# A two-level seven-product matmul on one core: the second level taken out

## The chip, the cores and the metric

One Trainium2 chip, one of its cores. The metric is device time in microseconds of one execution. The kernel before has a median of 891.07 us in 3 runs (890.15 to 894.06). One execution was also profiled; all rows below come from it.

## What is computed

One layer of a hybrid encoder block over 1024 tokens of width 1024. The part that the change touches is the input projection, a 1024 x 7200 matrix:

```
h = rmsnorm(x, norm_g)
proj = einsum('bsd,de->bse', h, w_in)
(q, k, v, z_a, lr_f, lr_b, b_gate, c_gate, h_c, z_c) = split(proj)
o   = gla_direction(q, k, v, g_f) + flipped gla_direction(... g_b)   # 4 heads, chunks of 64
y_a = rmsnorm(o) * silu(z_a)
y_c = b_gate * (conv3(c_gate * h_c) + conv_b) * silu(z_c)
out = rmsnorm(x + einsum('bse,ed->bsd', concat(y_a, y_c), w_out))
```

## The kernel before, in words

The program has four stages. First x is scaled, transposed and split into float32r high and low parts, the blocks `hb[d][s]` (d: half of the 1024 input columns, s: half of the 1024 tokens), and head 0 and 1 of v are multiplied directly. Second, `value_pair` (L468) multiplies heads 2 and 3 of v. Third, the loop at L687 to L694 multiplies everything else in 12 "quads": 8 for the convolution (c_gate and h_c, then z_c and b_gate), 4 for attention (q and k, then z). Fourth come attention and the output projection, from L698 on.

Every product of two float32 matrices is made of three float32r matmuls, high by high, high by low and low by high (`product`, L392), so a product over four blocks of 128 input columns takes 12 matmuls, each with a 128x128 weight block and 512 tokens moving (a "wide" matmul).

The input projection uses a seven-product scheme (Winograd's form of Strassen's). A pair (`pair`, L417) takes two blocks of 128 output columns, e = 0 and 1, in which `a00` and `a01` are the two halves of the input columns of block 0 (tile `raw0`) and `a10`, `a11` those of block 1 (`raw1`). Sums of these weights (`comb`, L421: `s1`, `s2` and two in `tmp` tiles) and sums of the blocks `hb` (`t1` to `t4`, made once) are multiplied. VectorE adds the products out of PSUM with `plus` (L444, at L445). ScalarE rounds each weight part to its high half (L153), GpSimd subtracts to get the low half (L154); `part` (L207) does both, into a ring of 6 tiles for each half. SyncE's queue loads the weights (L82), 4 raw tiles in all, and stores results; it takes its entries in order.

One of a pair's seven products, `a01` by `b10`, goes straight into the result `c00` = `a00` by `b00` + `a01` by `b10`. In the kernel before, this product has a second level: `quad` (L558) takes two pairs at once, whose `a01` together form a matrix of 512 input columns by 256 output columns, and `second` (L519) applies the same seven-product scheme to it, with the quarters of the block `hb[1][0]` and three quarter sums of it (`tt1`, `tt2`, `tt3`, made in `later_sums` at L668 to L675 and behind `value_pair` at L680 to L685). These seven products have 256 tokens moving (a "narrow" matmul) and 2 blocks of input columns, so 6 narrow matmuls each, 42 in a quad. Their results are the tiles `r`, which each pair adds to its first product (L458).

`second` holds four PSUM banks `bx`, `by`, `bz`, `bw` of a rotation of six (`bank6`, L401: names pa, pb, pc, two of each). `bx`, `by` and `bw` are used twice. The sixth narrow product writes `by` again, so PE must wait until VectorE has read the first result out of it at L542; the fifth must wait for ScalarE's copy at L540:

```
        product(by, first_(o1), t2, True, True)
        V.tensor_tensor(p1, by, p1, ALU.add)
        ...
        product(by, o3, t4, True, True)
        V.tensor_tensor(r[1][:, lo], by, u, ALU.add)
```

Behind each convolution quad come the gates of one head and direction (`gates`, L582): 4 wide matmuls over 64 rows (L591), then ScalarE and VectorE work on them. The scheduler of the language sets each engine's order; VectorE, ScalarE, GpSimd and the DMA queue run what stands in that order, one after the other.

Of the kernel before, what the change touches and what calls it, by code (L numbers as in the profile page):

```python
# [37 lines left out]
def tile_hybrid_gla_shortconv(ctx, tc, x, norm_g, w_in, w_gk_f, b_gk_f, w_gk_b, b_gk_b,  # L38
# [168 lines left out]
    def part(src, e_lo=G, late=False):  # L207
        pool, name, bufs = (resp, "w", 2) if late else (ws, "a", 6)
        hi, lo = (pool.tile([P, 4, P], F32R, name=f"{name}_{i}", bufs=bufs) for i in ("hi", "lo"))
        hi, lo = (a[:, 0:src.shape[1]] for a in (hi, lo))  # L210
        split(hi, lo, src, A, e_lo)
        return hi, lo
# [140 lines left out]
    def less(f, x, y, blk, behind):  # L353
        V.tensor_tensor(f, x, y, ALU.subtract)
        split_later(behind, *blk, f)


    quarters = [tuple(a[:, 2 * d:2 * d + 2, 256 * s_:256 * s_ + 256] for a in hb[1][0])
                for d in range(2) for s_ in range(2)]
    tt1 = tuple(a.rearrange("p c t -> p (c t)").rearrange("p (c t) -> p c t", c=2) for a in y_pair())  # L360
    tt2, tt3 = (tuple(tp.tile([P, 2, 256], F32R, name=f"tt{i}_{n}") for n in ("hi", "lo")) for i in (2, 3))

    beside = sums()
    with tc.manual_schedule():
        for _ in values(1, wv):
# [26 lines left out]
    def product(ps, a, b_, start, stop):  # L392
        n = a[0].shape[1]
        for k in range(n):
            for j, (x0, x1) in enumerate(((0, 0), (0, 1), (1, 0))):
                T.matmul(ps, a[x0][:, k], b_[x1][:, k], start=start and k == 0 and j == 0,  # L396
                         stop=stop and k == n - 1 and j == 2, skip_group_check=not start)
# [7 lines left out]
    def load(col):  # L405
        return weights(w_in[:, :, col:col + P])
# [7 lines left out]
            with tc.issue_after(behind.ins):  # L414
                beside.pop(0)()

    def pair(raw0, raw1, take, c2=None, mid=None, step=lambda behind: None):  # L417

        a00, a01, a10, a11 = raw0[:, 0:4], raw0[:, 4:8], raw1[:, 0:4], raw1[:, 4:8]

        def comb(f, x0, x1, op):  # L421
            V.tensor_tensor(f, x0, x1, op)  # L422
            return f

        def t4_():
            return tmp().rearrange("p (c e) -> p c e", e=P)

        o00 = part(a00)
        if c2 is None:
            o01 = part(a01)  # L430
        s1 = comb(s_tile(), a10, a11, ALU.add)
        s2 = comb(s_tile(), s1, a00, ALU.subtract)
        os2 = part(s2)
        os3 = part(comb(t4_(), a00, a10, ALU.subtract))
        os1 = part(s1)
        o11 = part(a11)
        os4 = part(comb(t4_(), a01, s2, ALU.subtract))

        def whole_product(a, b_):
            ps = bank6()  # L440
            product(ps, a, b_, True, True)
            return ps

        def plus(f, ps, x):  # L444
            step(V.tensor_tensor(f, ps, x, ALU.add))  # L445
            return f

        pa = whole_product(o00, b00)
        p1 = tmp()
        A.copy(p1, pa)  # L450
        if mid is not None:
            mid()
        if c2 is None:
            product(pa, o01, b10, False, True)
            c2 = tmp()
            A.copy(c2, pa)
        else:
            V.tensor_tensor(c2, pa, c2, ALU.add)  # L458
        take(0, 0, c2)
        plus(p1, whole_product(os2, t2), p1)  # L460
        w = plus(tmp(), whole_product(os3, t3), p1)
        p5 = whole_product(os1, t1)
        take(1, 1, plus(tmp(), p5, w))
        plus(p1, p5, p1)
        take(1, 0, plus(w, whole_product(o11, t4), w))
        take(0, 1, plus(p1, whole_product(os4, b11), p1))
# [49 lines left out]
            V.tensor_tensor(x[i], ps, x[i], ALU.add)  # L516
            out_v(h0, 1, i, x[i])

    def second(x, y, h):  # L519

        b00, t1, t2, t3, b10, b11, t4 = h
        a00, a01, a10, a11 = x[:, 0:2], x[:, 2:4], y[:, 0:2], y[:, 2:4]
        f, g = s_tile(), s_tile()
        s2, s1, s3, s4 = f[:, 0:2], f[:, 2:4], g[:, 0:2], g[:, 2:4]
        o0 = part(x)
        V.tensor_tensor(s1, a10, a11, ALU.add)
        V.tensor_tensor(s2, s1, a00, ALU.subtract)
        o1 = part(f)
        V.tensor_tensor(s3, a00, a10, ALU.subtract)
        V.tensor_tensor(s4, a01, s2, ALU.subtract)  # L530
        o2 = part(g)
        o3 = part(a11)
        first_, last_ = (lambda o: tuple(a[:, 0:2] for a in o)), (lambda o: tuple(a[:, 2:4] for a in o))
        r = [wk.tile([P, 512], F32, name="r2", bufs=2) for _ in range(2)]
        lo, hi = slice(0, 256), slice(256, 512)
        w = tmp()
        p1, u = w[:, lo], w[:, hi]
        bx, by, bz, bw = (bank6()[:, lo] for _ in range(4))
        product(bx, first_(o0), b00, True, True)
        A.copy(p1, bx)  # L540
        product(by, first_(o1), t2, True, True)
        V.tensor_tensor(p1, by, p1, ALU.add)  # L542
        product(bz, first_(o2), t3, True, True)
        V.tensor_tensor(u, bz, p1, ALU.add)
        product(bw, last_(o1), t1, True, True)
        V.tensor_tensor(r[1][:, hi], bw, u, ALU.add)
        product(bx, last_(o0), b10, False, True)
        A.copy(r[0][:, lo], bx)
        product(by, o3, t4, True, True)
        V.tensor_tensor(r[1][:, lo], by, u, ALU.add)  # L550

        def finish():
            product(bw, last_(o2), b11, False, True)
            V.tensor_tensor(r[0][:, hi], bw, p1, ALU.add)

        return *r, finish

    def quad(cols_a, take_a, cols_b, take_b):  # L558
        xa, xb = load(cols_a[0]), load(cols_b[0])
        ra, rb, finish = second(xa[:, 4:8], xb[:, 4:8], h2)  # L560
        pair(xa, load(cols_a[1]), take_a, ra, finish, step)
        pair(xb, load(cols_b[1]), take_b, rb)

    def to_dram(dsts):
        def take(e, half, ap):
# [93 lines left out]
    def later_sums():  # L659

        behind = []
        for c in range(4):
            f = joined(t2, c, tmp)
            minus(joined(hb[1][0], c, tmp), f, t4, c, f, behind)
            if c % 2 == 1:
                yield
        finish_low(behind)
        f = [tmp().rearrange("p (c t) -> p c t", c=2) for _ in range(3)]  # L668
        for f_, i in zip(f, (0, 1, 3)):
            whole(f_, quarters[i])  # L670
        less(f[0], f[1], f[0], tt1, behind)
        yield
        less(f[1], f[2], f[1], tt3, behind)
        less(f[0], f[2], f[0], tt2, behind)
        finish_low(behind)  # L675
        yield

    with tc.issue_after(last_mm[0].ins):
        value_pair(2, 3, o00, o01, os2, a00, a01, a10, a11, s2, later_sums())
    f = [wk.tile([P, 512], F32, name="r2", bufs=2).rearrange("p (c e) -> p c e", c=2) for _ in range(2)]  # L680
    whole(f[0], tt2)
    whole(f[1], quarters[2])
    V.tensor_tensor(f[0], f[1], f[0], ALU.subtract)
    split(*quarters[1], f[0])
    h2 = quarters[0], tt1, tt2, tt3, quarters[2], quarters[3], quarters[1]  # L685

    for j in range(CW // P):  # L687
        u, *first_ = conv_u(j)
        args = *first_, *conv_y(j, u)
# [378 lines left out]
```

## Time and profile before

| | |
|---|---|
| median of 3 runs | 891.07 us (890.15 to 894.06) |
| the profiled execution, its own time | 889.61 us |
| its span, first to last instruction | 887.9 us |
| TensorE (PE) matmuls busy | 860.0 us, 97% |
| VectorE (DVE) busy | 704.4 us, 79% |
| ScalarE (ACT) busy | 393.7 us, 44% |
| GpSimd (POOL) busy | 421.6 us, 47% |
| mean granted TensorE clock | 0.995 |

In the profile a matmul's bar reaches from its start to its modelled end, and a matmul starts before the one ahead of it has ended. So the time that a matmul costs in a full stream is read from the distance between two starts, not from the length of a bar; and the idle time printed behind a row, in brackets, is counted from the modelled end of the matmul ahead. PEld are the weight loads, which run beside the matmuls. A row with "<-" names what the engine waited for. Times are in us from the span's start.

### The profile page before, as it was taken

The page shows a single profiled execution, that of the slowest core. Times are in us where ns is not written, and L with a number is a line of the kernel's source. Part 1 is how long each engine was busy: PE and PEld are TensorE (multiplying, and loading weights), DVE is VectorE, ACT ScalarE, POOL GpSimd, SP SyncE. Part 2 cuts the span into 40 slices and gives each one's busy share as a digit, 9 for nine tenths or more (in the row PEclk, how much of TensorE's full clock was granted, in tenths as well). Part 3 has the DMA queues.
Part 4 walks back from the last instruction along what each step waited for, and adds up shares of the span by engine and source line. Part 5 has one row for each costly group of instructions (what it writes and reads, how often), then busy time and mean ns, then how long its engine had stood idle before and what let it go on. Part 6 is the DMA issues. An engine that isn't in the chain of part 4 may idle for free.

```text
span 887.9 us, 12975 instructions
## 1 busy us (share of the span) xinstructions
PE 860.0 (97%) x4452; PEld 722.8 (81%) x4452; DVE 704.4 (79%) x1301; ACT 393.7 (44%) x823; POOL 421.6 (47%) x374
## 2 busy tenths in 40 slices
PE   7999989999999999999999999999999999999996
PEld 6999978887787878788878888887878787888885
DVE  5889968788888798888887566667799989975754
ACT  4634323454636263444544233433455446542453
POOL 3423657586767675766766554520112222222231
PEclk9999999999999999999999999999999999999998
DMA  8511331223132322222244433469665434410122
GB/s 301 115 54 49 96 120 48 82 62 118 49 95 72 96 66 77 72 72 72 72 132 129 131 96 105 135 210 392 226 205 190 131 113 135 131 37 24 42 78 95
DMA packets 102164, 100.35 MB, mean 113 GB/s; under 512 B 10705, under 2 KB 82385, under 8 KB 101586
## 3 DMA queue, kind: packets, MB, share of 16 engines
q1 hardware_dynamic: 102098, 99.53, 35.4%
q8 instruction: 35, 0.57, 0.3%
q14 instruction: 31, 0.25, 0.1%
HBM read 71.20 MB, written 28.31 MB: 112 GB/s over the span
## 4 chain that ended last, share of the span: by engine, by line
PE 76%; DVE 17%; issue 3%; DMA 2%; ACT 1%; SPq 0%; POOLq 0%; POOL 0%; DVEq 0%; ACTq 0%
PE out L734 16%; PE pa L396 16%; PE pb L396 15%; PE pc L396 15%; PE po L891 4%; PE out L223 3%; PE pu L936 2%; DVE tmp L445 1%; DVE tmp L649 1%; DVE s L422 1%; DVE tmp L320 1%; DMA b<-b_dram 1%; PE out L291 1%; DMA xt<-in_x 1%; PE pk L928 1%
## 5 line engine op out<-in xcount | busy, mean ns | idle before, releaser
L154 POOL TENSOR_TENSOR a_lo<-s,a_hi 128x512 fp32r<-128x512 f32 x74 | 116.2, 1575 | 54.8 <-ACT a_hi L153 54.5
L154 POOL TENSOR_TENSOR a_lo<-raw,a_hi 128x512 fp32r<-128x512 f32 x84 | 111.0, 1325 | 22.1 <-ACT a_hi L153 18.4
L154 POOL TENSOR_TENSOR a_lo<-tmp,a_hi 128x512 fp32r<-128x512 f32 x48 | 70.3, 1464 | 103.9 <-ACT a_hi L153 84.6
L148 POOL TENSOR_TENSOR rs<-rs,mhalf 128x1 f32<-128x1 f32 x48 | 28.7, 598 | 143.1 <-DVE rs L147 135.7
L734 PE MATMUL out<-a_hi,y_hi 128*128 128x512 f32 x192 | 88.7, 462 | 0.5 <-ACT y_hi L153 0.5
L153 ACT CAST a_hi<-raw 128x512 fp32r<-128x512 f32 x108 | 63.8, 596 | 56.4 <-PE pc L396 15.1
L153 ACT CAST a_hi<-tmp 128x512 fp32r<-128x512 f32 x48 | 29.8, 620 | 120.2 <-DVE tmp L422 98.9
L734 PE MATMUL out<-a_hi,y_lo 128*128 128x512 f32 x192 | 77.0, 401 | 0.0
L734 PE MATMUL out<-a_lo,y_hi 128*128 128x512 f32 x192 | 76.8, 400 | 0.0
L846 POOL TENSOR_TENSOR kt<-kt,k 128x256 f32<-128x256 f32 x32 | 26.3, 822 | 95.5 <-ACT kt L843 72.2
L153 ACT CAST a_hi<-s 128x512 fp32r<-128x512 f32 x74 | 45.0, 617 | 50.7 <-PE pa L396 17.5
L396 PE MATMUL pb<-h_hi,a_hi 128*128 128x512 f32 (+1 forms) x128 | 48.3, 377 | 4.8 <-DVE tmp L542 4.2
L396 PE MATMUL pc<-h_hi,a_hi 128*128 128x512 f32 (+1 forms) x128 | 47.6, 372 | 2.9 <-DVE tmp L542 2.6
L396 PE MATMUL pa<-h_hi,a_hi 128*128 128x512 f32 (+1 forms) x128 | 47.6, 372 | 2.8 <-DVE tmp L542 2.8
L396 PE MATMUL pb<-h_lo,a_hi 128*128 128x512 f32 (+1 forms) x128 | 47.1, 368 | 0.0
L396 PE MATMUL pb<-h_hi,a_lo 128*128 128x512 f32 (+1 forms) x128 | 47.0, 367 | 0.0
L396 PE MATMUL pa<-h_lo,a_hi 128*128 128x512 f32 (+1 forms) x128 | 46.6, 364 | 0.0
L396 PE MATMUL pc<-h_lo,a_hi 128*128 128x512 f32 (+1 forms) x128 | 46.6, 364 | 0.0
L396 PE MATMUL pc<-h_hi,a_lo 128*128 128x512 f32 (+1 forms) x128 | 46.5, 363 | 0.0
L396 PE MATMUL pa<-h_hi,a_lo 128*128 128x512 f32 (+1 forms) x128 | 46.5, 363 | 0.0
L736 DVE TENSOR_TENSOR res<-out,res 128x512 f32<-128x512 f32 x48 | 32.9, 686 | 12.4 <-PE out L734 12.4
L734 PEld LDWEIGHTS out<-a_hi,y_lo 128*128 128x128 f32 x192 | 36.3, 189 | 7.8
(341 smaller groups left out, 2696.6 us busy)
## 6 DMA issues: line engine op xcount, KB each, us to landing
raw<-in_w_in SPq DMA_DIRECT2D x56, 512.0 KB, 3.9
raw<-in_w_out SPq DMA_DIRECT2D x16, 512.0 KB, 3.8
xt<-in_x SPq DMA_DIRECT2D x8, 512.0 KB, 8.2
yc_dram<-tmp SPq DMA_DIRECT2D x16, 256.0 KB, 2.0
b_dram<-u SPq DMA_DIRECT2D x8, 512.0 KB, 2.6
z_dram<-tmp SPq DMA_DIRECT2D x16, 256.0 KB, 2.6
s<-yc_dram SPq DMA_DIRECT2D x16, 256.0 KB, 3.9
raw<-in_x SPq DMA_DIRECT2D x8, 512.0 KB, 6.3
```

Of the source, the lines that this page charges most:

```text
L148: G.tensor_tensor(rs, rs, mhalf, ALU.pow)
L153: (e_hi.copy if e_hi is A else e_hi.tensor_copy)(hi, src)
L154: e_lo.tensor_tensor(lo, src, hi.bitcast(F32), ALU.subtract)
L223: last_mm[0] = T.matmul(ps, h_tile(a, c, t), wv[c // 4][w_][:, c % 4, :], start=part == 0 and c == 0, stop=part == 2 and c == ND - 1)
L291: T.matmul(lps, lrw[:, c, :], hb[c // 4][half][j][:, c % 4, :], start=c == 0 and j == 0, stop=c == ND - 1 and j == 1)
L320: V.tensor_tensor(f, blk[0].bitcast(F32)[:, c], blk[1].bitcast(F32)[:, c], ALU.add)
L396: T.matmul(ps, a[x0][:, k], b_[x1][:, k], start=start and k == 0 and j == 0, stop=stop and k == n - 1 and j == 2, skip_group_check=not start)
L734: T.matmul(ps, a[:, j, :], w, start=j == 0 and i == 0, stop=j == 3 and i == 2)
L736: V.tensor_tensor(res[t][:, cs], ps, (xr if row0 == NT else res[t])[:, cs], ALU.add)
L846: G.tensor_tensor(kk, kk, k4, ALU.mult)
L891: T.matmul(o, l, m, start=j == 0, stop=j == len(mm) - 1)
L936: T.matmul(pu[:, d], ks[:, d], r["v"][:, t], start=True, stop=True)
```

## The change

`second` goes, with the quarters, the quarter sums `tt1` to `tt3`, and the tiles `r`. Each pair makes `a01` by `b10` itself, as one product of 12 wide matmuls in a bank of its own from the rotation, and VectorE adds it to `p1`, the ScalarE copy of the first product. With it each pair splits its own `a01` (`o01`).

```
-    quarters = [tuple(a[:, 2 * d:2 * d + 2, 256 * s_:256 * s_ + 256] for a in hb[1][0])
-                for d in range(2) for s_ in range(2)]
-    tt1 = ...
-    tt2, tt3 = (tuple(tp.tile([P, 2, 256], F32R, ...
...
         o00 = part(a00)
-        if c2 is None:
-            o01 = part(a01)
+        o01 = part(a01)
...
         pa = whole_product(o00, b00)
         p1 = tmp()
         A.copy(p1, pa)
-        if mid is not None:
-            mid()
-        if c2 is None:
-            product(pa, o01, b10, False, True)
-            c2 = tmp()
-            A.copy(c2, pa)
-        else:
-            V.tensor_tensor(c2, pa, c2, ALU.add)
-        take(0, 0, c2)
+        c00 = tmp()
+        V.tensor_tensor(c00, whole_product(o01, b10), p1, ALU.add)
+        take(0, 0, c00)
...
-    def second(x, y, h):
...
     def quad(cols_a, take_a, cols_b, take_b):
         xa, xb = load(cols_a[0]), load(cols_b[0])
-        ra, rb, finish = second(xa[:, 4:8], xb[:, 4:8], h2)
-        pair(xa, load(cols_a[1]), take_a, ra, finish, step)
-        pair(xb, load(cols_b[1]), take_b, rb)
+        pair(xa, load(cols_a[1]), take_a, step)
+        pair(xb, load(cols_b[1]), take_b)
...
         finish_low(behind)
-        f = [tmp().rearrange("p (c t) -> p c t", c=2) for _ in range(3)]
-        for f_, i in zip(f, (0, 1, 3)):
-            whole(f_, quarters[i])
-        less(f[0], f[1], f[0], tt1, behind)
         yield
-        less(f[1], f[2], f[1], tt3, behind)
-        less(f[0], f[2], f[0], tt2, behind)
-        finish_low(behind)
...
-    f = [wk.tile([P, 512], F32, name="r2", bufs=2).rearrange("p (c e) -> p c e", c=2) for _ in range(2)]
-    whole(f[0], tt2)
-    whole(f[1], quarters[2])
-    V.tensor_tensor(f[0], f[1], f[0], ALU.subtract)
-    split(*quarters[1], f[0])
-    h2 = quarters[0], tt1, tt2, tt3, quarters[2], quarters[3], quarters[1]
```

The scheduler then sets the engines' orders anew. Three places show what moves. The first is VectorE at the end of the first convolution quad, where the second begins. In the kernel before (L445 adds products, L593 reads the gates out of PSUM, L648 and L649 finish the gated output, L422 are the weight sums, and L542, L544, L546 read the narrow products):

```order
L445 TENSOR_TENSOR tmp<-pc,tmp 128x512
L445 TENSOR_TENSOR tmp<-pa,tmp 128x512
L593 TENSOR_SCALAR u<-out,bgk 128x512
L648 SCALAR_TENSOR_TENSOR th<-th,tmp 128x512
L593 TENSOR_SCALAR u<-out,bgk 128x512
L649 SCALAR_TENSOR_TENSOR tmp<-th,tmp 128x512
L542 TENSOR_TENSOR tmp<-pc,tmp 128x256
L422 TENSOR_TENSOR tmp<-raw 128x512
L544 TENSOR_TENSOR tmp<-pa,tmp 128x256
L422 TENSOR_TENSOR tmp<-raw,s 128x512
L546 TENSOR_TENSOR r_1865<-pb,tmp 128x256
```

The same place in the changed kernel (its L540, L595, L596 are L593, L648, L649 of before; its L438 and L445 add products, L558 and L552 are the scan of the gates):

```order
L438 TENSOR_TENSOR tmp<-pa,tmp 128x512
L438 TENSOR_TENSOR tmp<-pb,tmp 128x512
L540 TENSOR_SCALAR u<-out,bgk 128x512
L595 SCALAR_TENSOR_TENSOR th<-th,tmp 128x512
L540 TENSOR_SCALAR u<-out,bgk 128x512
L596 SCALAR_TENSOR_TENSOR tmp<-th,tmp 128x512
L445 TENSOR_TENSOR tmp<-pa,tmp 128x512
L438 TENSOR_TENSOR tmp<-pb,tmp 128x512
L558 TENSOR_TENSOR u<-u 128x512
```

The gate and output work stands where it stood. What comes behind it is no longer the read of a bank that PE needs for its sixth narrow product, but the add of the quad's second wide product.

The second place is VectorE near the end of `value_pair`. In the kernel before (L499, L503, L506 add products of `value_pair`; L351, L354, L329, L334 make the quarter sums; L526 begins `second`):

```order
L499 TENSOR_TENSOR tmp<-pb,tmp 128x512
L354 TENSOR_TENSOR tmp<-tmp 128x512
L329 TENSOR_TENSOR y_lo<-tmp,y_hi 128x512
L503 TENSOR_TENSOR tmp<-pc,tmp 128x512
L354 TENSOR_TENSOR tmp<-tmp 128x512
L329 TENSOR_TENSOR tt_lo<-tmp,tt_hi 128x512
L503 TENSOR_TENSOR tmp<-pa,tmp 128x512
L334 TENSOR_TENSOR tt_lo<-tmp,tt_hi 128x512
L506 TENSOR_TENSOR tmp<-pb,tmp 128x512
L351 TENSOR_TENSOR r_1461<-tt_hi,tt_lo 128x512
L351 TENSOR_TENSOR r_1462<-h_hi,h_lo 128x512
L526 TENSOR_TENSOR s<-raw 128x256
```

In the changed kernel (its L486, L490, L493 are L499, L503, L506 of before, its L416 is L422):

```order
L486 TENSOR_TENSOR tmp<-pb,tmp 128x512
L334 TENSOR_TENSOR h_lo<-tmp,h_hi 128x512
L490 TENSOR_TENSOR tmp<-pc,tmp 128x512
L490 TENSOR_TENSOR tmp<-pa,tmp 128x512
L493 TENSOR_TENSOR tmp<-pb,tmp 128x512
L416 TENSOR_TENSOR s<-raw 128x512
L416 TENSOR_TENSOR s<-s,raw 128x512
L493 TENSOR_TENSOR tmp<-pc,tmp 128x512
```

The quarter sums are gone, and the first weight sums of the first quad have moved ahead, to between the adds of the fourth product of `value_pair`.

The third place is SyncE's DMA queue around the end of the first quad. In the kernel before (L654 stores the gated convolution, L613 the gates, L82 loads weights):

```order
L654 DMA yc_dram<-tmp 128x512 x2
L82 DMA raw<-in_w_in 128x8x128 x2
L613 DMA b_dram_79<-u 128x1024
L82 DMA raw<-in_w_in 128x8x128 x2
L654 DMA yc_dram<-tmp 128x512 x2
```

In the changed kernel (L601 and L560 are the two stores):

```order
L601 DMA yc_dram<-tmp 128x512
L82 DMA raw<-in_w_in 128x8x128
L601 DMA yc_dram<-tmp 128x512
L560 DMA b_dram_79<-u 128x1024
L82 DMA raw<-in_w_in 128x8x128 x3
```

One of the two loads that stood behind both stores now stands between them, the other ahead of them, and the store of the gates has three loads behind it, of which the third is for one quad later.

## Rows read from the trace of the kernel before

**Rows 1.** The page: busy time of the engines; DMA issues of weights (us to landing).
```profile
PE 860.0 (97%) x4452; PEld 722.8 (81%) x4452; DVE 704.4 (79%) x1301; ACT 393.7 (44%) x823; POOL 421.6 (47%) x374
...
raw<-in_w_in SPq DMA_DIRECT2D x56, 512.0 KB, 3.9
```

**Rows 2.** The chain in order of time: start, length, what; second convolution quad, then attention.
```profile
200.91 3.72 PE pa L396 x18
...
208.09 2.75 PE pc L396 x12
...
241.65 3.73 PE pb L396 x18
...
484.25 3.67 PE pb L396 x18
...
522.37 3.60 PE pc L396 x18
```

**Rows 3.** PE's timeline, start of the second convolution quad: start, length, what, [idle before].
```profile
194.73 0.40 PE L396 MATMUL pb<-h_hi,a_lo 128*128 128x512 f32 x1
...
196.17 0.39 PE L396 MATMUL pc<-h_hi,a_hi 128*128 128x256 f32 x1
...
196.87 0.28 PE L396 MATMUL pc<-h_hi,a_lo 128*128 128x256 f32 x1
196.99 0.28 PE L396 MATMUL pa<-tt_hi,a_hi 128*128 128x256 f32 x1
...
199.12 0.28 PE L396 MATMUL pc<-h_hi,a_hi 128*128 128x256 f32 x1
...
199.72 0.28 PE L396 MATMUL pc<-h_hi,a_lo 128*128 128x256 f32 x1
200.91 0.39 PE L396 MATMUL pa<-h_hi,a_hi 128*128 128x256 f32 x1 [0.92 <-DVE tmp L542]
201.14 0.28 PE L396 MATMUL pa<-h_lo,a_hi 128*128 128x256 f32 x1
```

**Rows 4.** DVE's timeline at the same place, and at the end of `value_pair`.
```profile
199.39 1.14 DVE L649 SCALAR_TENSOR_TENSOR tmp<-th,tmp 128x512 f32<-128x512 f32 x1
200.45 0.41 DVE L542 TENSOR_TENSOR tmp<-pa,tmp 128x256 f32<-128x256 f32 x1
...
118.43 0.41 DVE L542 TENSOR_TENSOR tmp<-pb,tmp 128x256 f32<-128x256 f32 x1
```

**Rows 5.** PE's timeline: end of `value_pair`, first quad; then the first matmul behind the last quad.
```profile
110.92 0.28 PE L479 MATMUL pc<-a_lo,h_hi 128*128 128x256 f32 x1
...
113.05 0.28 PE L396 MATMUL pb<-tt_hi,a_lo 128*128 128x256 f32 x1
114.23 0.36 PE L396 MATMUL pc<-tt_hi,a_hi 128*128 128x256 f32 x1 [0.90 <-ACT a_hi L153]
...
116.30 0.28 PE L396 MATMUL pa<-h_hi,a_lo 128*128 128x256 f32 x1
118.89 0.58 PE L396 MATMUL pb<-h_hi,a_hi 128*128 128x256 f32 x1 [2.32 <-DVE tmp L542]
...
594.76 0.39 PE L734 MATMUL out<-a_hi,y_hi 128*128 128x512 f32 x1
```

**Rows 6.** Stretches: length, busy us of PE, PEld, DVE, ACT, POOL, granted clock, DMA share, GB/s.
```profile
118.50:123.00 4.50, 4.11 (x15) 3.62 (x16) 3.14 (x6) 1.54 (x4) 4.24 (x3) 0.62 0.56 152
119.00:592.00 473.00, 464.79 (x2222) 385.44 (x2223) 366.99 (x493) 202.48 (x333) 310.40 (x232) 1.00 0.31 92
```

**Rows 7.** Groups of DVE: xcount | busy us, mean ns | idle before; the quarter sums.
```profile
L354 DVE TENSOR_TENSOR tmp<-tmp 128x512 f32<-128x512 f32 x3 | 2.5, 845 | 0.0
L351 DVE TENSOR_TENSOR tmp<-h_hi,h_lo 128x512 f32<-128x512 f32 x3 | 2.3, 809 | 0.0
```

**Rows 8.** Groups of POOL on the page: low halves of the weights.
```profile
L154 POOL TENSOR_TENSOR a_lo<-s,a_hi 128x512 fp32r<-128x512 f32 x74 | 116.2, 1575 | 54.8 <-ACT a_hi L153 54.5
```

**Rows 9.** Waits of DVE: us in total, times, longest.
```profile
DVE s L526 <- DMA raw<-in_w_in: 15.1, 10, 3.4
```

More of the change, by code (lines that the diff above doesn't have):

```diff
@@ L355, in less @@
         split_later(behind, *blk, f)
-    quarters = [tuple(a[:, 2 * d:2 * d + 2, 256 * s_:256 * s_ + 256] for a in hb[1][0])
-                for d in range(2) for s_ in range(2)]
-    tt1 = tuple(a.rearrange("p c t -> p (c t)").rearrange("p (c t) -> p c t", c=2) for a in y_pair())
-    tt2, tt3 = (tuple(tp.tile([P, 2, 256], F32R, name=f"tt{i}_{n}") for n in ("hi", "lo")) for i in (2, 3))
     beside = sums()
@@ L415, in step, with pair @@
                 beside.pop(0)()
-    def pair(raw0, raw1, take, c2=None, mid=None, step=lambda behind: None):
+    def pair(raw0, raw1, take, step=lambda behind: None):
         a00, a01, a10, a11 = raw0[:, 0:4], raw0[:, 4:8], raw1[:, 0:4], raw1[:, 4:8]
@@ L517, in value_pair @@
             out_v(h0, 1, i, x[i])
-    def second(x, y, h):
[L521 to L556, printed above, removed]
     def quad(cols_a, take_a, cols_b, take_b):
         xa, xb = load(cols_a[0]), load(cols_b[0])
-        ra, rb, finish = second(xa[:, 4:8], xb[:, 4:8], h2)
-        pair(xa, load(cols_a[1]), take_a, ra, finish, step)
-        pair(xb, load(cols_b[1]), take_b, rb)
+        pair(xa, load(cols_a[1]), take_a, step)
+        pair(xb, load(cols_b[1]), take_b)
     def to_dram(dsts):
```

## The prediction

> **What bounds the kernel now.** I read the engines' busy times first. PE's matmuls are busy for 97% of the span [rows 1], so a change is worth what it does to PE's stream: the matmuls in it and the gaps between them. But a bar is longer than the step to the next start, so 97% hides gaps. I then read the chain of waits in order of time. From the first quad to the last it consists of PE's products, 2.75 us for each one of 12 wide matmuls [rows 2], broken at each convolution quad by a piece of VectorE work. PE's timeline at such a break [rows 3] shows the price of a matmul and of the wait. Twelve wide matmuls in 2.75 us are 0.229 us each. From 196.99 to 199.12 stand 18 narrow ones, 0.118 us each: half the columns, half the time. Then PE starts nothing from 199.72 to 200.91, and what it waits for is L542 on VectorE. VectorE's timeline [rows 4] says why: L542 stands behind the gate and output work, the last of it L649 at 199.39, and comes at 200.45. The bank that it reads was full at about 197.70 (the product's first matmul at 196.99 and six steps of 0.118). So VectorE was 2.8 us behind, and `second` wants the bank back after only three other narrow products, 3 x 6 x 0.118 = 2.1 us.
>
> The first quad is worse [rows 5]: 1.18 us from 113.05 to 114.23 and 2.59 us from 116.30 to 118.89, where a step of 0.118 was due. After the second of these waits the granted clock is 0.62 in the stretch from 118.5 to 123 [rows 6], so part of it ran at 1.2 GHz instead of 2.4; the engine had stood idle just before.
>
> **The change, part by part.** *Products.* A quad loses 42 narrow matmuls, 42 x 0.118 = 4.96 us, and gains 24 wide ones, 24 x 0.229 = 5.50 us [rows 2, 3]. That is 0.54 us more in each of 12 quads, 6.5 us in all, and it lies wholly on the path, since PE is the path. A bound from below is nothing less than this: both steps are measured in this stage at the same clock.
>
> For a stream of weight loads and matmuls the Trainium skill's page "TensorE: Matmul & The Clock Gate", section "Back-to-back issue gap", gives about 81 ns for 128 columns and about 131 ns for 512. On a line between them a narrow matmul is an estimated 98 ns, and the exchange would save 1.0 us in a quad instead of costing something. The trace disagrees: 229 ns for 512 columns and 118 for 256, nearly in proportion.
>
> *Waits.* The reuse of `bx`, `by` and `bw` goes, and with it both waits, for L542 and for L540. Each product now has its own bank out of six, and a bank comes round after five other products, 5 x 2.75 = 13.75 us, where VectorE was 2.8 us behind. I put the new bank wait at nothing. Its cover is those 13.75 us; with no cover at all it would again cost about what the old one did.
>
> *Quarter sums.* Near the end of `value_pair` VectorE loses six wide sums worth 2.5 + 2.3 us [rows 7] and the splits and sums that follow them. PE waits there for VectorE (118.43 for the first L542 [rows 4]), and the order shows the weight sums of the first quad moved ahead into `value_pair`. That is more than the two waits of 1.06 and 2.47 us that PE has there, so I let them go. If this cover is too thin, the first quad keeps some 5 us, with the slow clock.
>
> *Splits and adds.* In a quad the four splits of `second` give way to two, its four weight sums and its narrow evictions go, and the two adds of its results become two adds of `p1`. VectorE is busy 367 of 473 us of this stage and GpSimd 310 [rows 6], and both get less to do, so this costs nothing; PE's 2.75 us for a product covers a split of 1.58 us [rows 8]. No gain is put down for it either.
>
> *Loads.* The queue carries the same bytes. The order of loads and stores shifts, but loads still stand about a quad ahead, near 40 us, and land in 3.9 us [rows 1]. Cost nothing; the bound is a rival below.
>
> *The sum* is made over the whole stretch, because that counts every wait once. The first product could start at 110.92 + 0.12 = 111.04, and the first matmul behind the quads starts at 594.76 [rows 5]: 483.7 us now. After: 12 quads of 14 products, 168 x 2.75 = 462.0 us. To it come eight sets of gates; from 194.73 to 196.17 such a set takes 1.44 us less the 0.23 of the matmul ahead [rows 3], so 8 x 1.21 = 9.7 us. Together 471.7 us, which is 12.0 us less. As 6.5 us of matmuls are added, the waits that go must be worth 18.5 us. A check by quads: a convolution quad takes 241.65 - 200.91 = 40.74 us and would take 14 x 2.75 + 1.21 = 39.71; an attention quad takes 522.37 - 484.25 = 38.12 us and would take 38.50 [rows 2]. So the convolution quads gain a microsecond each, the attention quads, which hardly wait, lose 0.4, and the largest single piece, near 5 us, is the first quad. The rest of the program starts earlier and is otherwise left as it is.
>
> The profiled execution took 889.61 us, so its sum is 877.6. The median of the runs lies 1.46 us above that execution, and I keep this distance: **879.1 us**.
>
> **Rivals.**
>
> *The loads come late.* VectorE already waits 15.1 us in 10 times for the weights of the next quad, at most 3.4 [rows 9], and PE doesn't notice, since parts are made ahead. With a load between two stores, and three behind the store of the gates, the wait could pass on to PE. At 1.5 us in each of eight convolution quads it takes 12 us, and the time is 891. For it speaks the moved order, against it the lead of a quad. It decides when a load is issued less than its 3.9 us and a sum and split ahead of need.
>
> *VectorE's backlog only moves.* This is the case on the slow side. If PE's waits are not the banks' but VectorE's own lateness at a quad's end, then the first product whose bank still holds an unread result waits in place of the narrow one, the 18.5 us come back, and the 6.5 us of added matmuls are all that is left: 891.1 + 6.5 = 897.6 us. The place is the third or fourth product behind the gates. It needs VectorE to be over 13.75 us late, and the rows show 2.8; for it speaks that the gates and the output work still stand ahead of the first adds in VectorE's order.
>
> *The first quad keeps its waits.* VectorE reaches the first L542 only at 118.43 [rows 4], 7 us after `value_pair`; if the weight sums still come late, 5 us stay: 884.1 us.
>
> *Wide and narrow matmuls cost the same in the new order.* If weight loads set the pace, each at 0.118 us, a quad would save 18 x 0.118 = 2.1 us on products instead of paying 0.54, and the time would be 879.1 - 32 = 847 us. The wide products of the same stage, at 0.229, speak against it. The page named above would have it partly so.
>
> That the change doesn't do what it says is excluded: the order of the changed program has the wide matmuls in the place of the narrow ones.
>
> **How the numbers follow.** The forecast gets 0.85, late loads 0.05, the moved backlog 0.04, the first quad's waits 0.05, equal cost of matmuls 0.01. The range: gates could cost as little as four plain steps, 0.92 us, which takes off 2.3 us, and the runs reach 0.9 us below their median: 875.5 at the low end. At the high end stands the first quad's rival with a little scatter: 884.5. A measurement of this kernel can tell about 0.5% from no change, 4.5 us, so faster means under 886.6. Faster: 0.85 + 0.05 + 0.01 = 0.91; no change: 0.05; slower: 0.04.
>
> **What would show it.** Right: in the profile after, PE has 216 matmuls fewer, the chain of waits runs through the quads as products of 2.75 us without VectorE pieces, conv quads are 39.7 us apart and attention quads 38.5, no wait of PE names L542 or its successor, and the granted clock no longer falls at the first quad. Wrong: a new wait of PE behind the gates, on a weight part or a bank; a product that takes longer than 2.75 us; or a last stage that is longer than before and gives the gain back.

## The result and the profile after

The changed kernel takes 879.61 us (median of 4 runs, 879.14 to 880.01). The kernel before, on the same chip, takes 892.57 us (4 runs, 890.15 to 894.13). The ratio is 0.9849, interval 0.9822 to 0.9876. Predicted were 879.1 us. The profiled execution after took 879.14 us, with a span of 877.4 us.

The page after, first the busy times (as in [rows 1]), then the share of the chain by engine:

```profile
PE 859.9 (98%) x4236; PEld 713.9 (81%) x4236; DVE 644.3 (73%) x1181; ACT 374.1 (43%) x771; POOL 396.2 (45%) x349
...
PE 90%; DVE 5%; DMA 3%; issue 1%; ACT 1%; SPq 0%; POOLq 0%; POOL 0%; DVEq 0%; ACTq 0%
```

PE has 4452 - 4236 = 216 matmuls fewer and is busy for the same 860 us, so its busy time does not show the change: bars overlap, they count none of the pauses, and before they also hold slow steps and slow first matmuls behind waits. VectorE lost 60 us of work.

The chain in order of time, the rows that answer to [rows 2] (start, length, what):

```profile
111.70 2.77 PE pa L390 x12
114.47 2.75 PE pb L390 x12
...
191.08 2.97 PE pb L390 x12
194.05 2.75 PE pc L390 x12
...
230.88 2.95 PE pa L390 x12
...
270.66 2.97 PE pc L390 x12
...
578.37 2.75 PE pb L390 x12
581.11 2.75 PE pc L390 x12
583.86 4.50 PE out L667 x20
```

No piece of VectorE stands between the quads any more. Convolution quads are 39.80 and 39.78 us apart. A product behind the gates has 2.95 to 2.97 us in the chain, which counts to the modelled end of a matmul; from its first start to that of the next product it takes 2.86 to 2.88. The other products keep 2.75.

PE's waits after, with the largest total first (us in total, times, longest). None of them is at a quad's line, L390:

```profile
PE po L824 <- DVE at L811: 3.0, 9, 0.8
PE pc L237 <- POOL mask_b L120: 2.3, 1, 2.3
PE pa L185 <- DVE xt L178: 1.4, 1, 1.4
```

Stretches of the trace after (columns as in [rows 6]): the first quad's beginning, the whole quad stage, the rest:

```profile
118.50:123.00 4.50, 4.50 (x21) 3.69 (x20) 0.95 (x2) 1.06 (x2) 1.85 (x2) 1.00 0.00 0
111.50:583.70 472.20, 472.20 (x2051) 383.60 (x2049) 324.02 (x393) 187.83 (x291) 286.81 (x210) 1.00 0.32 95
583.70:877.40 293.70, 281.72 (x1369) 229.31 (x1367) 231.83 (x659) 138.06 (x393) 63.26 (x88) 1.00 0.41 139
```

The stage from the first product to the first matmul behind the quads takes 472.2 us, in which PE is busy all the time and the granted clock is 1.00. Before it was 483.6 (from the first product at 111.19), and the clock at the first quad 0.62.

Where the 11.4 us went is read from PE's timelines, from the first product of a quad to the first product of the next. The gates lie within. All lengths are in us. The runs of the experiments stand in the same table, and its last column gives the shortest and the longest of six quads:

| kernel | median | first quad | second | third to eighth |
|---|---|---|---|---|
| before | 892.4 | 44.75 | 40.23 | 40.43 to 41.25 |
| changed | 879.61 | 39.68 | 39.79 | 39.78 to 39.80 |
| e2_no_quarter_sums | 887.22 | 39.75 | 40.19 | 40.43 to 41.04 |
| e1_own_bank | 888.42 | 42.57 | 39.24 | 40.16 to 41.52 |
| e10_bank_and_no_sums | 884.66 | 39.11 | 39.23 | 40.11 to 40.88 |
| e6_first_quad_alone | 891.12 | 39.68 | 46.44 | 39.61 to 40.80 |
| e4_quarter_sums_kept | 878.81 | 39.68 | 39.79 | 39.78 to 39.80 |
| e3_same_bank | 894.46 | 39.99 | 40.12 | 41.73 to 41.77 |
| e13_four_banks | 879.86 | 39.68 | 39.84 | 39.79 to 40.14 |
| e14_two_banks | 921.86 | 42.42 | 46.16 | 44.55 to 44.60 |

The median of before is that of 23 runs. From 44.75 to 39.68 the first quad gains 5.1 us. The next seven together gain 6.4 (284.97 before, 278.53 after), and the four attention quads together lose 0.1 (153.85 and 153.95).

### The profile page after: what moved, and what is told of

Same layout as the page of the kernel before. It is cut to its first block, busy times and chain, and to the rows that moved or that the text cites. A ratio compares the mean times of both kernels' runs of the same rounds, so it can differ in the third digit from the quotient of the medians.

```text
span 877.4 us, 12286 instructions
## 1 busy us (share of the span) xinstructions
PE 859.9 (98%) x4236; PEld 713.9 (81%) x4236; DVE 644.3 (73%) x1181; ACT 374.1 (43%) x771; POOL 396.2 (45%) x349
## 4 chain that ended last, share of the span: by engine, by line
PE 90%; DVE 5%; DMA 3%; issue 1%; ACT 1%; SPq 0%; POOLq 0%; POOL 0%; DVEq 0%; ACTq 0%
PE pb L390 18%; PE pc L390 18%; PE pa L390 18%; PE out L667 16%; PE out L223 5%; PE po L824 3%; PE pu L869 2%; PE pc L466 2%; PE pb L466 2%; PE pa L466 1%; PE out L538 1%; DMA b<-b_dram 1%; DMA k<-k_dram 1%; PE out L291 1%; DMA xt<-in_x 1%
## 5 line engine op out<-in xcount | busy, mean ns | idle before, releaser
L154 POOL TENSOR_TENSOR a_lo<-s,a_hi 128x512 fp32r<-128x512 f32 x50 | 74.4, 1488 | 18.8 <-ACT a_hi L153 16.4
L416 DVE TENSOR_TENSOR s<-raw 128x512 f32<-128x512 f32 x24 | 29.1, 1214 | 50.2 <-DMA raw<-in_w_in 49.8
L390 PE MATMUL pc<-h_hi,a_lo 128*128 128x512 f32 x128 | 50.4, 394 | 0.0
L390 PE MATMUL pb<-h_hi,a_lo 128*128 128x512 f32 x128 | 50.4, 393 | 0.0
L390 PE MATMUL pa<-h_hi,a_lo 128*128 128x512 f32 x128 | 50.4, 393 | 0.0
L390 PE MATMUL pa<-h_lo,a_hi 128*128 128x512 f32 x128 | 50.2, 393 | 0.0
L390 PE MATMUL pb<-h_lo,a_hi 128*128 128x512 f32 x128 | 50.2, 393 | 0.0
L390 PE MATMUL pc<-h_lo,a_hi 128*128 128x512 f32 x128 | 50.2, 392 | 0.0
L390 PE MATMUL pb<-h_hi,a_hi 128*128 128x512 f32 x128 | 50.1, 392 | 0.0
L390 PE MATMUL pc<-h_hi,a_hi 128*128 128x512 f32 x128 | 50.1, 392 | 0.0
L390 PE MATMUL pa<-h_hi,a_hi 128*128 128x512 f32 x128 | 50.0, 391 | 0.0
L438 DVE TENSOR_TENSOR tmp<-pa,tmp 128x512 f32<-128x512 f32 x48 | 32.5, 685 | 22.7 <-PE pa L390 22.1
L438 DVE TENSOR_TENSOR tmp<-pc,tmp 128x512 f32<-128x512 f32 x48 | 32.5, 686 | 20.0 <-PE pc L390 19.5
```

The source lines that it names most:

```text
L154: e_lo.tensor_tensor(lo, src, hi.bitcast(F32), ALU.subtract)
```

## The experiments

### The first quad: quarter sums or banks

**e2_no_quarter_sums.** The kernel before without them.

```
-        f = [tmp().rearrange("p (c t) -> p c t", c=2) for _ in range(3)]
-        less(f[0], f[1], f[0], tt1, behind)
...
-    h2 = quarters[0], tt1, tt2, tt3, quarters[2], quarters[3], quarters[1]
+    h2 = quarters[0], quarters[1], quarters[2], quarters[3], quarters[2], quarters[3], quarters[1]
```

> The kernel before without the making of the quarter sums: quarters of the block itself stand in for them, so seven narrow products of the same size are made of other data, and the quarter sums are left out of the computation. Theory (the sums hold VectorE up ahead of the first quad): the waits of 1.06 and 2.47 us at the first quad and the slow clock behind them go, about 5 us, ratio 0.9945; the other quads keep their 40.7 us. Rival (the first quad waits for banks as the others do): its L542 wait shrinks only to the 1.1 us of the other quads, about 2 us gained, ratio 0.998.

Measured: 887.22 us (886.03 to 888.14, 6 runs), ratio 0.9932 [0.9908, 0.9955]. The first quad falls to 39.75; the others keep their waits, now named L540, which is L542 of before:

```profile
PE pa L394 <- DVE tmp L540: 2.8, 3, 1.0
PE pc L394 <- DVE tmp L540: 2.6, 3, 1.0
PE pb L394 <- DVE tmp L540: 2.3, 3, 1.0
```

So the quarter sums are what makes the first quad long in the kernel before, 5.0 us of it.

**e4_quarter_sums_kept.** The changed kernel, which still makes the quarter sums and uses none of them.

```
+        less(f[0], f[1], f[0], tt1, behind)
+        less(f[1], f[2], f[1], tt3, behind)
+        less(f[0], f[2], f[0], tt2, behind)
...
+    V.tensor_tensor(f[0], f[1], f[0], ALU.subtract)
+    split(*tt1, f[0])
```

> The changed kernel with the quarter sums still made as in the kernel before and then not used (the last of them is written over another quarter sum). Theory (their VectorE time ahead of the first quad is what cost there): the weight sums of the first quad come some 8 us later, PE waits 1 to 4 us at the first quad, time 881 to 884. Rival (the first quad waited for the bank alone): 879 to 880, no wait of PE at the first quad.

Measured: 878.81 us (878.12 to 881.25, 5 runs), ratio 0.9841 [0.9814, 0.9867]: the time of the changed kernel, so the rival was right. VectorE's timeline there (L421 are weight sums, L508 adds a product of `value_pair`, L450 and L443 are the first adds of the quad):

```profile
113.69 1.78 DVE L421 TENSOR_TENSOR s<-s,raw 128x512 f32<-128x512 f32 x1
115.39 0.68 DVE L508 TENSOR_TENSOR tmp<-pb,tmp 128x512 f32<-128x512 f32 x1
116.00 0.67 DVE L508 TENSOR_TENSOR tmp<-pc,tmp 128x512 f32<-128x512 f32 x1
117.91 0.69 DVE L450 TENSOR_TENSOR tmp<-pb,tmp 128x512 f32<-128x512 f32 x1 [1.24 <-issue]
```

VectorE works without a pause until 116.7, and PE doesn't wait: the first quad takes 39.68 us. The sums cost 5 us where narrow products need their results and their banks at once, and nothing here, where the first add of the quad is due only behind two wide products: VectorE is done at 116.7, and that add starts at 117.91.

### The waits of the other quads

**e1_own_bank.** The kernel before, with a seventh bank turn for the sixth narrow product.

```
-        product(by, o3, t4, True, True)
-        V.tensor_tensor(r[1][:, lo], by, u, ALU.add)
+        by2 = bank6()[:, lo]
+        product(by2, o3, t4, True, True)
+        V.tensor_tensor(r[1][:, lo], by2, u, ALU.add)
```

> The kernel before, with one thing altered: the sixth narrow product goes into a bank of its own, not into the second one's again. Theory (the bank's reuse makes PE wait for L542): that wait, 1.07 us and 0.11 us of slower restart in a convolution quad, goes, so eight quads give about 9 us back; ratio to the kernel before near 0.990, and PE's rows show no wait for L542 there. Rival (VectorE is late and its lateness only moves): PE waits as long at the next place, for ScalarE's copy L540 or for another bank, and the ratio is 0.998 to 1.002.

Measured: 888.42 us (885.77 to 891.67, 12 runs), ratio 0.9943 [0.9922, 0.9965]. The wait for L542 is gone, but the third to eighth quad stay as long as before (244.9 us together, 244.7 before), since PE now waits one product earlier, for ScalarE's copy at L540, 0.85 to 1.61 us in each quad from the fourth to the ninth. PE's timeline of this run at the longest of these waits:

```profile
279.97 0.39 PE L396 MATMUL pc<-h_hi,a_hi 128*128 128x256 f32 x1 [1.61 <-ACT tmp L540]
280.20 0.28 PE L396 MATMUL pc<-h_lo,a_hi 128*128 128x256 f32 x1
```

and ScalarE's at the same place (L648 is the tanh of the quad ahead, L593 reads the gates):

```profile
278.45 0.63 ACT L648 ACTIVATE th<-tmp 128x512 f32<-128x512 f32 x1 [2.27 <-DVE tmp L445]
278.99 0.67 ACT L593 ACTIVATE u<-out,bgk 128x512 f32<-128x512 f32 x1
279.56 0.36 ACT L540 COPY tmp<-pc 128x256 f32<-128x256 f32 x1
```

The copy stands behind a tanh that waits 2.27 us for VectorE's last add of the quad ahead (2.11 us one quad earlier). Of the 4.0 us of this run the first two quads give 3.2 (2.2 and 1.0).

**e10_bank_and_no_sums.** Both edits together.

> The kernel before with both single edits, the sixth narrow product in a bank of its own, and the quarter sums left out (quarters stand in for them, so the results are of other numbers). Alone they took 4.0 and 5.2 us from 892.4. If they remove different waits, both together take about 9 us: 883 us. Rival: they remove the same wait of the first quad, and both together take 5 to 6 us: 887 us. What is then still missing to the 879.6 us of the change, 3.5 us or more with 6.5 us of added products on top, is the wait for ScalarE's copy at the fifth narrow product.

Measured: 884.66 us (881.8 to 887.95, 6 runs), ratio 0.9918 [0.989, 0.9945], 7.6 us off the 892.23 of the kernel before on the same chip; alone the edits took 4.0 and 5.2. The first quad is at 39.11 and gains little on e2; from the fourth to the eighth the quads are still at 40.73 to 40.88, each with a wait of 0.84 to 0.96 us for the copy. The stage is 2.8 us longer than in the changed kernel (475.0 and 472.2): 5.2 us more in the third to eighth quad (243.97 and 238.74 together), 2.4 us less in the other six, where narrow products are cheaper and only one such wait is left. The rest of the distance to the change, 2.3 us in the profiled execution, lies in the last stage, where the granted clock of this run was 0.57 from 601 to 605.

**e6_first_quad_alone.** The changed kernel's first quad, then 11 quads as in e1.

```
+        if len(quads) == 1:
+            pair(xa, load(cols_a[1]), take_a, step=step)
+            pair(xb, load(cols_b[1]), take_b, step=step)
+            return
```

> The changed kernel's single level in the first quad alone; the other 11 quads keep two levels in the order of the kernel before, the sixth narrow product with a bank of its own, and the quarter sums are made beside the first quad. If the first quad's waits of the kernel before (3.5 us in two of them, and the slow clock behind) come from the reuse of banks, and the waits for ScalarE's copy in the other quads (0.85 to 1.6 us in 6 to 8 of them) stay as in the run with the own bank alone, the time is that run's 888.4 less about 4: 884 us. Rival: the waits of the first quad only move to the second, where the narrow products now come for the first time: 888 us.

Measured: 891.12 us (889.47 to 893.13, 12 runs), ratio 0.9986 [0.9971, 1.0001]. The rival was right, and by more than it said: the second quad takes 46.44 us, with the longest wait of the run and slow steps behind it. PE's wait for ScalarE's copy (us in total, times, longest), and VectorE and ScalarE ahead of that copy, which ends at 159.04 (L691 makes a low half of the quarter sums, L654 is the tanh, L445 adds products):

```profile
PE pc L396 <- ACT tmp L539: 6.1, 3, 4.4
...
154.60 1.75 DVE L691 TENSOR_TENSOR h_lo<-tmp,h_hi 128x512 fp32r<-128x512 f32 x1
...
157.58 0.63 ACT L654 ACTIVATE th<-tmp 128x512 f32<-128x512 f32 x1 [2.33 <-DVE tmp L445]
```

In the kernel before, in the first quad, and here, in the second, narrow products right behind the quarter sums wait.

### How many banks the wide products need

**e3_same_bank.** The changed kernel with the second product added up in the bank of the first.

```
+        product(pa, o01, b10, False, True)
-        V.tensor_tensor(c00, whole_product(o01, b10), p1, ALU.add)
+        V.tensor_copy(c00, pa)
```

> The changed kernel, with the second product of a pair summed up in the bank of the first and not in a bank of its own; VectorE copies the sum out. Theory (a bank of its own matters, not only the single level): PE waits in each of 24 pairs until ScalarE has copied the first product, a copy of 0.58 us and its start, 0.8 to 1.1 us, with the gates ahead of it on ScalarE more; 20 to 30 us lost, time 900 to 910. Rival (the single level alone brings the gain): 879 to 882.

Measured: 894.46 us (893.42 to 897.63, 12 runs), ratio 1.0011 [0.9993, 1.0029]. The bank of its own is worth 14.9 us, more than the whole gain of the change, and less than the 20 to 30 us expected. The second product must wait for ScalarE's copy of the first. That copy stands behind the tanh, which waits only 0.26 us here, and behind the work on the gates, which ends at 198.99; it starts at 199.40. PE's waits for it (us in total, times, longest), each of which costs about 1.7 us from start to start and 0.11 more in the matmul behind it:

```profile
PE pa L390 <- ACT tmp L443: 10.7, 7, 1.5
```

**e13_four_banks and e14_two_banks.** The changed kernel with a shorter rotation.

```
-            ps = bank6()
+            turn_[0] += 1
+            ps = pq.tile([P, 512], F32, name=("pa", "pb")[turn_[0] % 2])
```

and, for two banks, `name="pa"` alone.

> The changed kernel with four PSUM banks in rotation for the quads' products in place of six: a bank comes round after three other products, 3 x 2.75 = 8.25 us, in place of 13.75. In the changed kernel's trace the latest eviction at the turn of a quad is ScalarE's copy, which ends at 199.07 where its product ended at 194.05, 5.0 us late. If that is what the cover has to hold, four banks cost nothing: 879.6 us. Rival: the evictions are later elsewhere, or lateness adds up over a quad, so that the cover of 13.75 us was needed: waits of PE for L438, L443 or L445 come up in the convolution quads, and the time is over 884 us.

> The same with two banks: a bank comes round after one other product, 2.75 us. If the eviction at the turn of a quad is 5.0 us late, PE waits about 2.3 us there, behind the first or second product, 8 times or more: 18 us, about 898 us, slower than the kernel before. Rival: ScalarE and VectorE are late there only because nothing needs them sooner (they stand in order behind the gates), and their order shifts with the banks: then the wait is under 0.5 us at each turn, and the time is below 884 us.

Measured: with four banks 879.86 us (878.51 to 882.39, 6 runs), ratio 0.9836 [0.9808, 0.9864], the time of six, and no wait of PE at the products. With two 921.86 us (921.49 to 922.01, 5 runs), ratio 1.03 [1.0272, 1.0329]. A cover of 8.25 us is enough and one of 2.75 is far too little. The loss is more than twice what was expected, and it lies elsewhere: not behind the gates, where ScalarE's copy was expected to be late, but 14 and 9 us ahead of a quad's end, and for adds of VectorE. There are two such waits in a convolution quad. PE's timeline shows them in the third quad, then in the eighth:

```profile
229.38 0.40 PE L390 MATMUL pa<-t_hi,a_lo 128*128 128x512 f32 x1
231.73 0.50 PE L390 MATMUL pa<-t_hi,a_hi 128*128 128x512 f32 x1 [1.95 <-DVE tmp L446]
...
232.94 0.63 PE L390 MATMUL pa<-t_lo,a_hi 128*128 128x512 f32 x1
233.37 0.63 PE L390 MATMUL pa<-t_hi,a_lo 128*128 128x512 f32 x1
...
236.59 0.50 PE L390 MATMUL pa<-t_hi,a_hi 128*128 128x512 f32 x1 [0.26 <-DVE tmp L439]
...
454.62 0.51 PE L390 MATMUL pa<-t_hi,a_hi 128*128 128x512 f32 x1 [1.98 <-DVE tmp L446]
...
459.51 0.50 PE L390 MATMUL pa<-t_hi,a_hi 128*128 128x512 f32 x1 [1.84 <-DVE tmp L439]
```

and, as a stretch, the 4 us behind the first of them:

```profile
232.00:236.00 4.00, 4.00 (x12) 3.05 (x11) 4.00 (x6) 0.85 (x2) 1.81 (x1) 0.57 0.00 0
```

Behind the wait of 1.95 us the steps are 0.43 us instead of 0.23: TensorE runs at its lower level, 1.2 GHz, for eight steps, 8 x 0.2 = 1.6 us. They don't make the quad longer, though. The second wait shrinks by as much, to 0.26 us, because VectorE's second add comes no sooner: the third to seventh quad, with slow steps, take 44.55 to 44.59 us, the eighth, without any, 44.60. Only in the second quad (46.16) and in the last (42.39, the one ahead 38.46), where no wait follows the slow steps, do these cost their 1.6 us. What VectorE did meanwhile is seen in its timeline of the same run:

```profile
229.88 1.20 DVE L416 TENSOR_TENSOR s<-raw 128x512 f32<-128x512 f32 x1 [1.75 <-DMA raw<-in_w_in]
230.99 0.68 DVE L446 TENSOR_TENSOR tmp<-pa,tmp 128x512 f32<-128x512 f32 x1
...
235.86 0.68 DVE L439 TENSOR_TENSOR tmp<-pa,tmp 128x512 f32<-128x512 f32 x1
```

The first add, which would free the bank, stands behind a weight sum that waits for its load; the second stands behind the convolution's own sums, from 231.59 on. The late load is the first rival of the prediction, which lies hidden in the changed kernel: VectorE's waits there, against 18.5 us before (15.1 at L526 in [rows 9] and 3.4 at L422):

```profile
DVE s L416 <- DMA raw<-in_w_in: 49.8, 22, 5.9
```

### What the exchange of products is worth alone

**e7_last_three.** The second level in the last three attention quads only. (One quarter of the block is overwritten by its sum before the second to ninth quad read it whole, so these compute with other numbers.)

```
+        if len(quads) <= 9:
+            pair(xa, load(cols_a[1]), take_a, step=step)
+            pair(xb, load(cols_b[1]), take_b, step=step)
+            return
```

> The changed kernel, with the second level only in the last three quads, all of attention, in the order of the kernel before but with a bank of its own for the sixth narrow product. In the kernel before an attention quad took 38.12 us, in the changed one 38.5. If attention quads hardly wait, three of them give back 3 x 0.38 to 3 x 0.54 us: 878.0 to 878.5 us against the changed kernel's 879.6. Rival: the wait for ScalarE's copy, seen when the sixth narrow product got its own bank, costs more than the exchange gives, and the time is 880 to 882.

Measured: 878.77 us (877.3 to 881.24, 6 runs), ratio 0.9852 [0.9827, 0.9877], which the runs can't tell from the changed kernel. The length of its last quads can, as the chain shows:

```profile
476.07 3.47 PE pa L396 x18
...
514.01 3.43 PE pc L396 x18
...
551.84 3.43 PE pb L396 x18
```

Two-level quads are 37.94 and 37.83 us apart and have no wait of PE; the same quads of the changed kernel, 14 plain products, take 38.45. The exchange is worth 0.51 and 0.62 us in a quad. The prediction's price was 0.54.

**e9_interleaved and e12_in_order_of_use.** If narrow products are cheaper by that much, an order without waits should beat both kernels. Each was tried in 11 quads, a narrow product or two between wide ones, and a bank for each.

```
+        A.copy(q, narrow(cols(o0, 0), c00))
+        add(r[0][:, lo], narrow(cols(o0, 2), c10), q)
+        step(add(p1, wide(os2, t2), base))
+        add(q, narrow(cols(o1, 0), t2_), q)
...
```

> The changed kernel, with the second level put back in 11 of the 12 quads, but in another order: each narrow product stands between two wide ones of the first pair, with a bank of its own, and the last one stands in the second pair; the quarter sums are made beside the first quad, which stays at one level. If the exchange of products is worth what the trace of before says (42 narrow at 0.118 against 24 wide at 0.229, 0.54 us in a quad) and if PE's waits came from the tight order of the narrow products alone, no wait comes back and 11 quads save 5.9 us against the changed kernel: about 873.7 us, faster than both. Rival: VectorE's added work (four weight sums, seven narrow evictions, two more adds in a quad) is what makes PE wait, whatever the order: then waits near 1 us come back in most quads, and the time is 880 to 890 us.

> The interleaved order again (the second level in 11 of the 12 quads, narrow products between wide ones, a bank for each), but with the weight parts made in the order in which the products use them, so that no part waits for a place in the ring of six behind a part that is used later. In the run e9_interleaved PE stood 8 us in each of several quads waiting for weight parts (23.5, 18.0 and 15.2 us in 8 waits for ScalarE's half alone). If that was the order of the parts, these waits go, and the exchange of products (0.54 us in a quad, in 11 quads) shows: about 873.7 us against the changed kernel's 879.6. Rival: with seven narrow products more, the engines that make the parts and empty the banks are late whatever the order; then waits of 1 us or more stay in most quads and the time is 885 us or more.

Measured: 996.62 us (994.71 to 998.45, 6 runs), ratio 1.1163 [1.1135, 1.1192], and 932.53 us (930.88 to 935.58, 6 runs), ratio 1.0441 [1.0412, 1.0471]. In the first PE waits for weight parts, which come in the wrong order for the ring of six:

```profile
PE pb L396 <- ACT a_hi L153: 23.5, 3, 8.0
PE pc L396 <- ACT a_hi L153: 15.2, 2, 7.6
```

In the second that wait is gone, and PE waits 2.8 to 4.2 us in each of eight quads for the copy of the first wide product:

```profile
PE pa L396 <- ACT tmp L563: 12.6, 3, 4.2
PE pc L396 <- ACT tmp L563: 11.2, 3, 4.2
PE pb L396 <- ACT tmp L563: 8.4, 2, 4.2
```

ScalarE's timeline there (L692 the tanh of the quad ahead, L646 the gates):

```profile
208.38 0.63 ACT L692 ACTIVATE th<-tmp 128x512 f32<-128x512 f32 x1 [4.59 <-DVE tmp L445]
...
210.69 1.28 ACT L646 ACT_TABLE_LOAD   x1
211.99 1.06 ACT L646 ACTIVATE u<-u 128x1024 f32<-128x1024 f32 x1
212.95 0.57 ACT L563 COPY tmp<-pa 128x512 f32<-128x512 f32 x1
```

It is once more the tanh, and now also the gates, ahead of the copy. The bank of that product comes round after one wide and four narrow products here, 2.75 + 4 x 0.7 = 5.6 us, and PE is back before the copy is made. Neither theory held: both orders lose more in waits than the products give. An order of ScalarE with the copy ahead of the gates wasn't tried. No version was found that is faster than the changed kernel beyond the scatter of the runs.

## Why the prediction was right, point by point

*Products.* +0.54 us in a quad was right; e7_last_three shows 0.51 and 0.62. The step of 0.229 holds in all 168 products. The rival of equal cost is out.

*The sum.* 471.7 us for the stage, measured 472.2. The half microsecond is made of two errors: a product behind a set of gates takes 2.86 to 2.88 us where 2.75 were put down, 1.0 us in eight, and the others, at 2.746, take 0.6 us less in all. Convolution quads were predicted at 39.71 and are at 39.78 to 39.80, attention quads at 38.50, and they are 14 plain products. All four of these together lost only 0.1 us instead of 1.5, since in the kernel before the first of them follows the last gates and still had both waits. The check by quads had missed that: seven quads at 1.03 us, near 5 for the first and four at -0.38 make 10.7 of the 12.0 us. The waits that went, with the slow clock and the slower first matmuls behind them, come to 483.6 - 472.2 + 6.5 = 17.9 us, where the prediction had 18.5. The low end of the range has a slip: 879.1 - 2.3 - 0.9 is 875.9 and not 875.5.

*The first quad.* Near 5 us was right, and e2_no_quarter_sums shows that the quarter sums caused it. The step's reason was only half right, though. It said that the waits go because VectorE loses this work; e4_quarter_sums_kept keeps the work, and the waits go all the same. They go because the first quad no longer asks for narrow results at once. In the first quad either is enough by itself.

*The waits of the other quads.* That both waits go, for L542 and for L540, was needed: e1_own_bank and e10_bank_and_no_sums take one away, the other comes, and most of these quads stay near 40.8.

*The new bank wait.* Nothing, as predicted. Its reason named VectorE, 2.8 us behind. The later engine is ScalarE: in the changed kernel's trace the copy of a quad's first product ends at 199.07, where the product ends at 194.05:

```profile
193.41 0.63 ACT L594 ACTIVATE th<-tmp 128x512 f32<-128x512 f32 x1 [0.26 <-DVE tmp L438]
...
198.49 0.58 ACT L443 COPY tmp<-pb 128x512 f32<-128x512 f32 x1
```

That is 5.0 us late, within 13.75 and within the 8.25 of four banks. The rival of a backlog that moves is what e14_two_banks and e3_same_bank show, at covers that the change doesn't have. In e14_two_banks it comes near a quad's end, and not at the third or fourth product. The Trainium skill's page "Perfetto Trace Analysis", section "Matmuls", asks that independent groups of matmuls rotate through different PSUM banks, so that emptying one overlaps the next; these runs agree, with 14.9 us for one more bank turn. Its section "Matmul Optimizations" asks for all 8 banks to be used; here four in the products' rotation do as well as six (879.86 and 879.61).

*Loads.* No cost to PE was right, but not because loads stand far enough ahead: VectorE waits 49.8 us for them, where it waited 18.5 before. The banks cover it, and where they don't, in e14_two_banks, it reaches PE.

*Around the stage.* The profiled time came out 879.14, not 877.6: 0.5 us is the stage, 0.5 what lies ahead of it (first product at 111.54 instead of 111.04 to 111.19), and the last stage is longer by about half a microsecond. The distance from the profiled execution to the median, 1.46 us before, is 0.47 after. These errors cancel by luck, so the median fits better than the steps.

## What to carry to other kernels

A cheaper product that frees its bank sooner also asks for the bank sooner, and what then counts is the latest in-order engine that empties banks, with everything that its queue holds ahead of that. Before saving matmuls on a full TensorE, compare the time until a bank comes round with the end of its latest eviction at the worst turn. Taking away one of two waits that hang on the same late work only moves PE to the other one. And a slow stretch of TensorE in front of a wait can cost nothing, so compare whole quads before giving it a price.

## What was not expected of the hardware

A wait of PE can be followed by slow steps, but not each one is. In e14_two_banks eleven waits of 1.84 to 1.98 us stand in the quads; behind seven of them the steps are soon 0.43 us, as in the stretch above at a granted clock of 0.57, and behind four, those at 454.62 and 459.51 among them, the clock stays at 1.00. Behind the 4.2 us in e12_in_order_of_use it was 0.62 from 213.5 to 217.5. Behind the waits of 1.5 us in e3_same_bank and of 1.61 us in e1_own_bank the steps from the second on were those of full speed. The page "TensorE: Matmul & The Clock Gate" of the Trainium skill, section "A second HAM failure mode: psum-queue depth-cycling", tells of a kernel that cycles through PSUM banks, in which TensorE idles shortly between groups of matmuls, the clock goes up and down, and throughput suffers from that. The two-bank run agrees that the clock falls behind such pauses, but not on the price: by the lengths of its quads only 3.2 of its 42 us, in the second and the last quad, are owed to slow steps, since in the others a wait would have filled that time.

A first matmul behind a wait or behind the 64-row matmuls of the gates takes 0.11 us more to the next start: 0.34 instead of 0.23 for a wide one (151.22 to 151.56 in the changed kernel), 0.23 instead of 0.12 for a narrow one [rows 3].
